# The causal mask moved from a matrix product to the row minimum, and q/k splits done for two heads at once, in a two-layer decoder trunk

## The chip, the cores and the metric

The kernel runs on one core of a Trainium2 chip. The metric is device microseconds of one execution of the whole program, the median of several. TensorE does the matrix products, VectorE, ScalarE and GpSimd the elementwise work, and SyncE issues the DMAs.

## The reference, cut to what matters

Two post-norm layers over 1024 tokens of width 1024. Layer 0 mixes tokens with differential attention, layer 1 with forgetting attention; each is followed by a gated MLP (2816 wide) with a causal convolution of width 3 on the gate branch. All is float32.

```python
def masked_softmax(scores, mask):
    s = jnp.where(mask, scores.astype(jnp.float32), -jnp.inf)
    return jax.nn.softmax(s, axis=-1)

# layer 0: 8 heads, each with 2 components of 64 dimensions
q = apply_rotary(...); k = apply_rotary(...)      # the first 16 dimensions of 64
s = jnp.einsum('bhcqd,bhckd->bhcqk', qb, k) * scale
p = masked_softmax(s, causal_mask(start, Q_BLOCK, S))
a = (p[:, :, 0] - lam * p[:, :, 1]).astype(v.dtype)
o = rms_norm(jnp.einsum('bhqk,bhkd->bqhd', a, v), subln_g) * (1.0 - lambda_init)

# layer 1: 16 heads of 64 dimensions, a forget gate per head and token
c = jnp.cumsum(log_f, axis=1).transpose(0, 2, 1)
s = (jnp.einsum('bhqd,bhkd->bhqk', qb, k) * scale + cb[..., :, None] - c[..., None, :])
p = masked_softmax(s, causal_mask(start, Q_BLOCK, S))

h = layer_norm(DEEPNORM_ALPHA * h + y, ...)       # y: attention output, then again the MLP's
```

## The kernel before, in words

**Float32 by halves.** A float32 factor is split into a high part, which TensorE's reduced float32 type holds exactly, and a low part, the rest. `split` (lines 83 to 91) does it: ScalarE copies the source into the high part (line 86), and VectorE subtracts that from the source (line 88, or line 90 where a scale is applied first). A float32 product is then three products, high x high, low x high and high x low (`mm3`, lines 97 to 99).

**Pairs.** The attention of a layer goes in 8 rounds (`attention`). A round works on two heads, in layer 0 on the two components of one head, and each of the two fills 64 of the 128 partitions. Round p does the scores, softmax and value products of pair p. Between them, in 48 steps of three products, it projects q, k and v of pair p + 1 (`project`, line 374), in halves of 512 tokens; in the last round the steps are products of the output projection. `tick`, `tock` and `steps` set how many steps stand between two score jobs. Work that must follow a projection is queued with a delay in steps (`after`, run by `pulse`): evacuation from PSUM one step later (`result`), and in layer 0 the DMAs that collect the rotary dimensions (`gather`), nine steps later the rotation (`turn`), fourteen later the split of q and k (`halves`). Weights come by DMA (`ahead`) and are split later (`ready`).

**Order.** Every engine takes its instructions in a fixed order, which a scheduler derives from the order in which the code is written. All DMAs of this part are issued by SyncE, on one queue, in order: a DMA that has to wait for an engine holds back those behind it.

**Scores.** For a pair there are five tiles of 128 x 1024: q of each head, with its high part on that head's 64 rows and its low part on the other 64 (`split_q`, two splits of 64 x 512 per half); k of each head, with the same high part on both halves of the rows, and one tile with the low parts of both (`split_k`, two splits and two ScalarE copies). Then `scores` (line 467) needs two products per 512 keys: the first (line 481) contracts high and low q together against the doubled high k, the second (line 482) high q, which GpSimd copies into a tile whose other rows are zero (`qz`, line 474), against low k. A third product (line 483) adds the mask, which is an identity times a 128 x 128 triangle, both bf16, to the diagonal block, the last 128 columns. Per layer that is 8 pairs x 2 heads x 8 query blocks = 128 score rows of 128 to 1024 keys.

**Softmax.** In layer 0 VectorE takes the negated row maximum (line 502), ScalarE the exponential. In layer 1 scores and mask have the opposite sign; VectorE adds the key's gate sum c, broadcast over 128 partitions by a DMA of 512 KB per head (`load_ck`), and takes the row minimum in one instruction (line 627), followed by a read of its accumulator into `nm`; two small subtractions (lines 629 and 630) take the query's gate sum in and out again. The gate sums themselves (`forget_sums`) are made early in layer 1 and go through DRAM (`cd`, line 598).

Of the kernel before, what the change touches and what calls it, by code (L numbers as in the profile page):

```python
# [19 lines left out]
P = 128  # L20
# [3 lines left out]
NP = 8  # L24
# [17 lines left out]
PIN = 1  # L42
PSF, PSN, PN17 = (0,), 3, 0
# [10 lines left out]
class Trunk:  # L54
# [64 lines left out]
    def consts(self):  # L119
# [5 lines left out]
        self.idb = cp.tile([P, P], BF16, name="idb")  # L125
        nc.vector.tensor_copy(self.idb, self.ident)
        self.mneg = cp.tile([P, P], BF16, name="mneg")
        nc.vector.tensor_copy(self.mneg, mask)
        self.mpos = cp.tile([P, P], BF16, name="mpos")
        nc.vector.tensor_scalar(self.mpos, mask, -1.0, None, op0=ALU.mult)  # L130
# [132 lines left out]
    def split_q(self, par, src, scale, sl):  # L263

        for st, r in zip(par, (0, 64)):
            self.split(st[r:r + 64, sl], st[64 - r:128 - r, sl], src[r:r + 64, :], scale)

    def split_k(self, par, src, sl):

        a, b, lo = par  # L270
        for st, r in ((a, 0), (b, 64)):
            s = src[r:r + 64, :]
            self.split(st[r:r + 64, sl], lo[r:r + 64, sl], s)
            self.nc.scalar.activation(st[64 - r:128 - r, sl], s, AF.Copy)


    def after(self, n, fn, *args):
        self.queue.append([n, partial(fn, *args)])

# [38 lines left out]
    def first_pair_rotary(self, t):  # L318
# [23 lines left out]
        for c in range(2):  # L342
# [7 lines left out]
            self.after(2 + 2 * c, self.turn_v, 0, c, dst[2], *t[5:], True)  # L350
        self.ahead(4)

    def first_pair(self, l, t):
# [4 lines left out]
        for c in range(2):  # L358
# [10 lines left out]
            if c:  # L369
                self.after(3, self.turn_v, l, c, dst, *t[5:], True)  # L370
            else:
                self.turn_v(l, c, dst, *t[5:])

    def project(self, l, p, t):
# [6 lines left out]
        for n, (s, c) in enumerate(order):  # L381
# [18 lines left out]
            if s == 2:  # L400
                self.after(D_EV + 2, self.turn_v, l, c, dst[2], *t[5:], True)
            if c:
                del self.w[i + s]

    def result(self, l, s, c, ps, dst, t):

        sl = slice(c * 512, c * 512 + 512)
        if dst is not None:
            self.nc.scalar.activation(dst[:, sl], ps, AF.Copy, scale=DH ** -0.5 if s == 0 else 1.0)
        elif s == 0:  # L410
            self.split_q(t[:2], ps, -DH ** -0.5, sl)
        else:
            self.split_k(t[2:5], ps, sl)

    def halves(self, dst, t, c):
        sl = slice(c * 512, c * 512 + 512)
        self.split_q(t[:2], dst[0][:, sl], None, sl)
        self.split_k(t[2:5], dst[1][:, sl], sl)
# [48 lines left out]
    def scores(self, q, kd, kl, r, qt, mask):  # L467
# [3 lines left out]
        h = r // 64  # L471
        qz = self.qz[h][self.nz[h] % 2]
        self.nz[h] += 1
        nc.gpsimd.tensor_copy(qz[r:r + 64, :], q[r:r + 64, qt * P:qt * P + P])  # L474
# [1044 lines left out]
```

## Time and profile before

| what | value |
| --- | --- |
| runs | 2517.57, 2517.7, 2519.43 us; median 2517.7 us |
| span of the profiled execution | 2518.0 us |
| TensorE busy over the span | 97% |
| layer 0's attention | about 45 to 535 us |
| layer 1's attention | about 1260 to 1805 us |
| SyncE issues | 244 MB on its queue |

The span is from the first to the last instruction of one execution. A row of the groups by line reads: line, engine, operation, output<-input by the program's names, partitions x elements and type, count; then busy time, mean ns of one; then the engine's idle time just before these instructions and what ended it. A row of the timeline reads: start, duration, engine, line, operation, and in brackets a wait that it ended. A row of the windows reads: the window, its length, then busy time and count for each engine.

### The profile page before, as it was taken

Reading aid. Unit: us, or ns where it says so; the run is one execution under the profiler, and the core shown is the slowest. Engines: PE = TensorE matmul, PEld = TensorE weight load, DVE = VectorE, ACT = ScalarE, POOL = GpSimd, SP = SyncE. Lnnn points to the kernel's source line nnn. Section 1 sums busy time; section 2 is a strip of 40 time slices with the busy share of each in tenths; the row PEclk is TensorE's granted clock in tenths of the full one; section 3 lists DMA queues with packets and bytes.
Section 4 is the critical chain, followed back from the end, with each engine's and each line's share of the span. In section 5 each row is a group of like instructions: output and inputs, shape, how many; then the busy total and the mean of one; then the engine's idle time right before and its main releaser. Section 6 shows DMA issues by size and latency. Waiting matters only on the chain. (4 is left out here: it accounts for less than half of the span.)

```text
span 2518.0 us, 33818 instructions
## 1 busy us (share of the span) xinstructions
PE 2450.5 (97%) x12059; PEld 2015.0 (80%) x12059; DVE 1966.9 (78%) x3794; ACT 1335.3 (53%) x2515; POOL 136.1 (5%) x314
## 2 busy tenths in 40 slices
PE   8999999999999999999999999999999999999998
PEld 6887777787888888878778888888877888888876
DVE  5787877989876676696868878888888667666978
ACT  5666666656544445434546656656465444445344
POOL 2001101101000000000100000000010000000000
PEclk9999999999999999999999999999999999999999
DMA  4111111422222223842311111114222222228622
GB/s 152 39 57 55 47 47 49 179 93 98 81 92 84 76 83 124 304 161 80 127 54 51 51 51 51 51 59 154 89 84 86 98 75 76 100 85 271 221 89 96
DMA packets 97402, 247.02 MB, mean 98 GB/s; under 512 B 14513, under 2 KB 21553, under 8 KB 97233
## 3 DMA queue, kind: packets, MB, share of 16 engines
q1 hardware_dynamic: 96720, 244.00, 28.3%
q8 instruction: 95, 1.56, 0.3%
q0 software_dynamic: 512, 0.85, 0.1%
q14 instruction: 75, 0.61, 0.1%
HBM read 190.93 MB, written 47.58 MB: 95 GB/s over the span
## 5 line engine op out<-in xcount | busy, mean ns | idle before, releaser
L97 PE MATMUL m<-xh,wh 128*128 128x512 f32 x768 | 321.5, 419 | 11.7 <-ACT xh L86 8.8
L98 PE MATMUL m<-xl,wh 128*128 128x512 f32 x768 | 303.4, 395 | 1.2 <-DVE xl L88 1.2
L99 PE MATMUL m<-xh,wl 128*128 128x512 f32 x768 | 304.0, 396 | 0.0
L97 PE MATMUL m<-xh,wo 128*128 128x512 f32 x656 | 255.6, 390 | 1.1 <-ACT pt L1029 0.7
L99 PE MATMUL m<-xh,wo 128*128 128x512 f32 x656 | 255.4, 389 | 0.3 <-DVE wo L88 0.3
L98 PE MATMUL m<-xl,wo 128*128 128x512 f32 x656 | 255.2, 389 | 0.0
L86 ACT ACTIVATE wo<-wg 128x512 fp32r<-128x512 f32 x168 | 106.4, 633 | 224.5 <-PE m L99 218.3
L97 PE MATMUL m<-q,wo 128*128 128x512 f32 x472 | 184.1, 390 | 0.0
L98 PE MATMUL m<-q,wo 128*128 128x512 f32 x472 | 183.8, 389 | 0.0
L99 PE MATMUL m<-q,wo 128*128 128x512 f32 x472 | 183.7, 389 | 0.0
L86 ACT ACTIVATE pt<-m 128x512 fp32r<-128x512 f32 (+1 forms) x240 | 129.5, 551 | 91.3 <-PE m L1303 71.2
L97 PEld LDWEIGHTS m<-xh,wh 128*128 128x128 f32 x768 | 145.7, 190 | 36.7 <-ACT xh L86 8.8
L99 PEld LDWEIGHTS m<-xh,wl 128*128 128x128 f32 x768 | 144.7, 188 | 31.2 <-DVE wl L88 0.6
L98 PEld LDWEIGHTS m<-xl,wh 128*128 128x128 f32 x768 | 145.6, 190 | 24.7 <-DVE xl L88 1.8
L86 ACT ACTIVATE wo<-t 128x512 fp32r<-128x512 f32 x132 | 82.7, 627 | 147.5 <-PE m L99 133.3
L88 DVE TENSOR_TENSOR pt<-m,pt 128x512 fp32r<-128x512 f32 (+1 forms) x240 | 149.6, 632 | 11.0 <-ACT pt L86 9.4
L88 DVE TENSOR_TENSOR wo<-wg,wo 128x512 fp32r<-128x512 f32 x168 | 115.4, 688 | 40.3 <-ACT wo L86 39.4
L97 PEld LDWEIGHTS m<-xh,wo 128*128 128x128 f32 x656 | 123.1, 188 | 27.7 <-ACT pt L1029 1.6
L99 PEld LDWEIGHTS m<-xh,wo 128*128 128x128 f32 x656 | 123.1, 188 | 26.7 <-DVE wo L88 1.2
L474 POOL CAST qz<-q 64x128 fp32r<-64x128 f32 x256 | 94.9, 372 | 910.1 <-PE s L483 832.8
L98 PEld LDWEIGHTS m<-xl,wo 128*128 128x128 f32 x656 | 123.1, 188 | 25.6
L86 ACT ACTIVATE oa<-ha 128x512 fp32r<-128x512 f32 x128 | 79.4, 624 | 112.6 <-PE s L99 57.7
(324 smaller groups left out, 6356.9 us busy)
## 6 DMA issues: line engine op xcount, KB each, us to landing
wst<-in_w SPq DMA_DIRECT2D x46, 512.0 KB, 3.3
t<-in_wi SPq DMA_DIRECT2D x44, 512.0 KB, 4.3
ad<-t SPq DMA_DIRECT2D x44, 512.0 KB, 3.5
ha<-ad SPq DMA_DIRECT2D x88, 256.0 KB, 5.5
wg<-in_wi SPq DMA_DIRECT2D x42, 512.0 KB, 3.3
wb<-in_wd SPq DMA_DIRECT2D x84, 256.0 KB, 3.3
pt<-in_wd SPq DMA_DIRECT2D x48, 256.0 KB, 3.8
wst<-in_wo SPq DMA_DIRECT2D x16, 512.0 KB, 3.3
```

Of the source, the lines that this page charges most:

```text
L86: nc.scalar.activation(hi, src, AF.Copy, scale=1.0 if scale is None else scale)
L88: nc.vector.tensor_tensor(lo, src, hi.bitcast(F32), op=ALU.subtract)
L97: mm(out, wh, xh, start=start, stop=False)
L98: mm(out, wh, xl, start=False, stop=False)
L99: mm(out, wl, xh, start=False, stop=stop)
L474: nc.gpsimd.tensor_copy(qz[r:r + 64, :], q[r:r + 64, qt * P:qt * P + P])
```

## The change

**Mask.** The third product goes in both layers. A constant tile `mask` of 128 x 1024 in bf16 holds zeros and, in its last 128 columns, the triangle. VectorE adds it to the scores and takes the row minimum in one instruction (`top`), the form that layer 1 had for its gate sums. Layer 0 now also has scores of the opposite sign, and its row maximum goes.

**Gate sums.** c is split into high and low part, and both go to DRAM. `load_c` brings the two rows of a head into rows 64 and 65 of the tile that holds this head's low k; the matching two rows of `qz` are ones, so the second score product contracts 66 rows and adds c. Each head of layer 1 thus has its own low tile with k on rows 0 to 63, the second being new (`kl`). The two small subtractions, the query's gate sum and the 16 broadcasts go.

**Splits.** `split_q` and `split_k` split both heads at once over 128 rows. `move_q` and `move_k` then bring the halves to where they belong, by DMAs of 64 x 512 from SBUF to SBUF: three for q and three for k per half of 512 tokens, in layer 1 four for k. They are queued two steps behind the split (`later`), and those of the first pairs are issued at once.

```diff
--- before
+++ after
@@ -40,6 +40,7 @@
 PIN = 1
+D_MV = 2
 PSF, PSN, PN17 = (0,), 3, 0
@@ -122,12 +123,9 @@
         nc.sync.dma_start(mask, i["mask"])
-        self.idb = cp.tile([P, P], BF16, name="idb")
-        nc.vector.tensor_copy(self.idb, self.ident)
-        self.mneg = cp.tile([P, P], BF16, name="mneg")
-        nc.vector.tensor_copy(self.mneg, mask)
-        self.mpos = cp.tile([P, P], BF16, name="mpos")
-        nc.vector.tensor_scalar(self.mpos, mask, -1.0, None, op0=ALU.mult)
+        self.mask = cp.tile([P, 1024], BF16, name="mask")
+        nc.gpsimd.memset(self.mask[:, :1024 - P], 0.0)
+        nc.vector.tensor_scalar(self.mask[:, 1024 - P:], mask, -1.0, None, op0=ALU.mult)
         self.qz = [[cp.tile([P, P], F32R, name=f"qz{h}{b}") for b in range(2)] for h in range(2)]
@@ -260,22 +258,48 @@
     def qtile(self, par):
         return self.qp.tile([P, 1024], F32R, tag=f"q{par}", name=self.nm("q"))
-    def split_q(self, par, src, scale, sl):
-        for st, r in zip(par, (0, 64)):
-            self.split(st[r:r + 64, sl], st[64 - r:128 - r, sl], src[r:r + 64, :], scale)
+    def split_q(self, par, src, lo, scale, sl):
+        x, y = par
+        self.split(x[:, sl], lo, src, scale)
+        return x[:, sl], y[:, sl], lo
+    def move_q(self, x, y, lo, l):
+        dma = lambda d, s: self.nc.sync.dma_start(d.bitcast(F32), s.bitcast(F32))
+        if l == 0:
+            dma(y[64:128], x[64:128])
+            dma(x[64:128], lo[0:64])
+            dma(y[0:64], lo[64:128])
+        else:
+            dma(y[0:64], x[64:128])
+            dma(x[64:128], lo[0:64])
+            dma(y[64:128], lo[64:128])
     def split_k(self, par, src, sl):
-        a, b, lo = par
-        for st, r in ((a, 0), (b, 64)):
-            s = src[r:r + 64, :]
-            self.split(st[r:r + 64, sl], lo[r:r + 64, sl], s)
-            self.nc.scalar.activation(st[64 - r:128 - r, sl], s, AF.Copy)
+        a, b, lo = [t[:, sl] for t in par[:3]]
+        self.split(a, lo, src)
+        return (a, b, lo, par[3][:, sl] if len(par) > 3 else None)
+    def move_k(self, a, b, lo, lo1):
+        dma = lambda d, s: self.nc.sync.dma_start(d.bitcast(F32), s.bitcast(F32))
+        dma(b[0:64], a[64:128])
+        dma(b[64:128], a[64:128])
+        dma(a[64:128], a[0:64])
+        if lo1 is not None:
+            dma(lo1[0:64], lo[64:128])
     def after(self, n, fn, *args):
         self.queue.append([n, partial(fn, *args)])
+    def later(self, fn, *args):
+        if self.fill is None:
+            fn(*args)
+        else:
+            self.after(D_MV, fn, *args)
     def step(self):
@@ -398,24 +422,28 @@
             if s == 2:
-                self.after(D_EV + 2, self.turn_v, l, c, dst[2], *t[5:], True)
+                self.after(D_EV + 2, self.turn_v, l, c, dst[2], *t[5:7], True)
             if c:
                 del self.w[i + s]
+            if l and c and s == 1:
+                self.after(D_EV + D_MV + 1, self.load_c, p, t)
     def result(self, l, s, c, ps, dst, t):
         if dst is not None:
-            self.nc.scalar.activation(dst[:, sl], ps, AF.Copy, scale=DH ** -0.5 if s == 0 else 1.0)
+            self.nc.scalar.activation(dst[:, sl], ps, AF.Copy, scale=-DH ** -0.5 if s == 0 else 1.0)
         elif s == 0:
-            self.split_q(t[:2], ps, -DH ** -0.5, sl)
+            lo = self.tp.tile([P, 512], F32R, tag="sq", name=self.nm("ql"), bufs=1)
+            self.later(self.move_q, *self.split_q(t[:2], ps, lo, -DH ** -0.5, sl), l)
         else:
-            self.split_k(t[2:5], ps, sl)
+            self.later(self.move_k, *self.split_k((*t[2:5], t[7]), ps, sl))
     def halves(self, dst, t, c):
         sl = slice(c * 512, c * 512 + 512)
-        self.split_q(t[:2], dst[0][:, sl], None, sl)
-        self.split_k(t[2:5], dst[1][:, sl], sl)
+        q, k = dst[0][:, sl], dst[1][:, sl]
+        self.later(self.move_q, *self.split_q(t[:2], q, q.bitcast(F32R), None, sl), 0)
+        self.later(self.move_k, *self.split_k(t[2:5], k, sl))
     def gather(self, dst, r, c):
@@ -464,24 +492,29 @@
                            v3[h][:, :, 64 - 64 * h:128 - 64 * h], t3[:, :, 64 * h:64 * h + 64])
-    def scores(self, q, kd, kl, r, qt, mask):
+    def scores(self, q, kd, kl, h, qt, l):
         nc = self.nc
-        h = r // 64
         qz = self.qz[h][self.nz[h] % 2]
         self.nz[h] += 1
+        r = 0 if l else 64 * h
         nc.gpsimd.tensor_copy(qz[r:r + 64, :], q[r:r + 64, qt * P:qt * P + P])
+        m = 66 if l else P
         ln = (qt + 1) * P
         for c in range((ln + 511) // 512):
-            n = min(512, ln - c * 512)
-            ks = slice(c * 512, c * 512 + n)
-            last = (c + 1) * 512 >= ln
+            ks = slice(c * 512, min(ln, c * 512 + 512))
             nc.tensor.matmul(sb[:, ks], q[:, qt * P:qt * P + P], kd[:, ks], start=True, stop=False)
-            nc.tensor.matmul(sb[:, ks], qz, kl[:, ks], start=False, stop=not last)
-        nc.tensor.matmul(sb[:, ln - P:ln], self.idb, mask, start=False, stop=True)
+            nc.tensor.matmul(sb[:, ks], qz[:m], kl[:m, ks], start=False, stop=True)
         return sb, ln
+    def top(self, sb, ln):
+        mn = self.small(tag="nm")
+        self.nc.vector.tensor_tensor_reduce(sb[:, :ln], sb[:, :ln], self.mask[:, 1024 - ln:], 1.0, BIG,
+                                            ALU.add, ALU.min, mn)
+        return mn
     def diff_jobs(self, p, t):
@@ -497,12 +530,11 @@
     def diff_scores(self, t, qt, j, pr, pts):
         nc = self.nc
-        sb, ln = self.scores(t[j], t[2 + j], t[4], 64 * j, qt, self.mneg)
-        nmx, lsum = self.small(tag="nm"), self.small(tag="ls")
-        nc.vector.tensor_reduce(nmx, sb[:, :ln], axis=AX.X, op=ALU.max, negate=True)
+        sb, ln = self.scores(t[j], t[2 + j], t[4], j, qt, 0)
+        mn, lsum = self.top(sb, ln), self.small(tag="ls")
         yield
         pt = self.tmp(pool=self.wp, tag="wst", bufs=2) if j else self.tmp(pool=self.pp, tag="p")
-        nc.scalar.activation(pt[:, :ln], sb[:, :ln], AF.Exp, bias=nmx, accum_out=lsum)
+        nc.scalar.activation(pt[:, :ln], sb[:, :ln], AF.Exp, bias=mn, scale=-1.0, accum_out=lsum)
         yield
@@ -586,7 +618,7 @@
         nc.vector.tensor_tensor_scan(c, self.ones, l, 0.0, op0=ALU.mult, op1=ALU.add)
-        self.c = c
+        self.c, self.cw8 = c, w
     def forget_sums(self):
@@ -594,17 +626,17 @@
         nc.vector.tensor_scalar(c, c, tb[:, 0:1], None, op0=ALU.add)
-        self.cd = self.dr.tile([16, 1024], F32, name="cd")
-        nc.sync.dma_start(self.cd.rearrange("h (b t) -> (h b) t", t=P), c)
-        tc = self.mbank()
-        nc.tensor.transpose(tc[:, :P], c, self.ident)
-        self.cq = self.cp.tile([P, 16, 8], F32, name="cq")
-        nc.vector.tensor_copy(self.cq.rearrange("p a b -> p (a b)"), tc[:, :P])
-    def load_ck(self, p, h):
-        ct = self.lp.tile([P, 1024], F32, tag="lg", name=self.nm("ck"))
-        self.nc.sync.dma_start(ct, self.cd[2 * p + h:2 * p + h + 1, :].broadcast_to([P, 1024]))
-        self.ck[p, h] = ct
+        self.cd = self.dr.tile([2, 16, 1024], F32, name="cd")
+        w = self.cw8
+        hl = [w[:, j * P:j * P + P].bitcast(F32R) for j in (5, 6)]
+        self.split(*hl, c)
+        for j in range(2):
+            nc.sync.dma_start(self.cd[j].rearrange("h (b t) -> (h b) t", t=P), hl[j].bitcast(F32))
+    def load_c(self, p, t):
+        for h in range(2):
+            self.nc.sync.dma_start(t[(4, 7)[h]][64:66, :].bitcast(F32), self.cd[:, 2 * p + h, :])
     def fox_jobs(self, p, t):
@@ -617,19 +649,8 @@
     def fox_scores(self, p, h, t, qt, pts):
         nc = self.nc
-        cq = self.cq[:, 2 * p + h, qt:qt + 1]
-        if qt == 0 and (p, h) not in self.ck:
-            self.load_ck(p, h)
-        ck = self.ck[p, h]
-        sb, ln = self.scores(t[h], t[2 + h], t[4], 64 * h, qt, self.mpos)
-        mn, lsum = self.small(tag="nm"), self.small(tag="ls")
-        nc.vector.tensor_tensor_reduce(sb[:, :ln], sb[:, :ln], ck[:, :ln], 1.0, BIG,
-                                       ALU.add, ALU.min, mn)
-        nc.vector.tensor_tensor(mn, cq, mn, op=ALU.subtract)
-        nc.vector.tensor_tensor(mn, cq, mn, op=ALU.subtract)
-        if qt == 7 and p < NP - 1:
-            self.load_ck(p + 1, h)
+        sb, ln = self.scores(t[h], t[2 + h], t[(4, 7)[h]], h, qt, 1)
+        mn, lsum = self.top(sb, ln), self.small(tag="ls")
         yield
@@ -653,12 +674,16 @@
         self.od = self.dr.tile([NP, P, 1024], F32, name=f"od{l}")
-        tiles = lambda p: [self.qtile((p + l) % 2) for _ in range(7)]
+        tiles = lambda p: [self.qtile((p + l) % 2) for _ in range(7)] + (
+            [self.lp.tile([P, 1024], F32R, tag="lg", name=self.nm("kl"))] if l else [])
         self.slabs = [self.i[f"w{l}"][s * NP + p] for p in range(NP) for s in range(3)]
         self.w, self.stage, self.queue = {}, {}, []
-        self.ofs, self.ck = {}, {}
+        self.ofs, self.fill = {}, None
         if l == 1:
+            for h in range(2):
+                for t in self.qz[h]:
+                    nc.gpsimd.memset(t[64:66, :].bitcast(F32), 1.0)
             self.gate_logits(0)
@@ -676,6 +701,7 @@
                         self.forget_sums()
+                        self.load_c(0, cur)
             total, acc, base = sum(j[0] + 1 + W_C for j in jobs) - (W_V * 10 if l == 0 else 0), 0, done
             def steps(goal):
```

In the tables of instructions below a name is a tile with its number; `L` is the line, which lies some 1 to 28 lines later after the change.

TensorE at the first score of layer 0 (`s` scores, `m` projection, `q` tiles of the pair, `ident,t` transposes of v). Before:

```order
L99 MATMUL m_514<-xh_258,wl_265 128x512
L481 MATMUL s_550<-q_117,q_115 128x128
L482 MATMUL s_550<-q_119,qz_278 128x128
L483 LDWEIGHTS idb
L483 MATMUL s_550<-mneg,idb 128x128
L97 MATMUL m_564<-xh_157,wh_510 128x512
```

After:

```order
L100 MATMUL m_511<-xh_258,wl_265 128x512
L98 MATMUL m_560<-xh_157,wh_507 128x512
L99 MATMUL m_560<-xl_158,wh_507 128x512
L100 MATMUL m_560<-xh_157,wl_508 128x512
L98 MATMUL m_560<-xh_161,wh_507 128x512
L99 MATMUL m_560<-xl_162,wh_507 128x512
L100 MATMUL m_560<-xh_161,wl_508 128x512
L478 MATMUL m_567<-ident,t_124 128x128 x3
L508 MATMUL s_547<-q_117,q_115 128x128
L509 MATMUL s_547<-q_119,qz_275 128x128
```

The mask product with its weight load is gone, and six products of the next projection and three transposes now stand ahead of the first score.

SyncE in round 3 of layer 0, from the rotation's return of the first half to the next weights (`t<-t` collects and returns rotary rows, `wst` weights). Before:

```order
L444 DMA t_2489<-t_2773 32x256 x2
L444 DMA t_2490<-t_2773 32x256 x2
L429 DMA t_2773<-t_2489 32x256
L431 DMA t_2773<-t_2489 16x256 x2
...
L106 DMA wst_2954<-in_w 128x1024
L429 DMA t_2773<-t_2490 32x256
L431 DMA t_2773<-t_2490 16x256 x2
```

After, with the moves of q (line 269) and k (line 287):

```order
L107 DMA wst_2890<-in_w 128x1024
L457 DMA t_2713<-t_2437 32x256
L459 DMA t_2713<-t_2437 16x256
L269 DMA q_2407<-q_2406 64x512
L269 DMA q_2407<-t_2437 64x512
L287 DMA q_2409<-q_2408 64x512 x2
L269 DMA q_2406<-t_2437 64x512
L459 DMA t_2713<-t_2437 16x256
L457 DMA t_2713<-t_2438 32x256
L287 DMA q_2408<-q_2408 64x512
L459 DMA t_2713<-t_2438 16x256 x2
L457 DMA t_2713<-t_2438 32x256
L459 DMA t_2713<-t_2438 16x256 x2
L107 DMA wst_2977<-in_w 128x1024
```

Six moves stand between and among the gathers of the second half, ahead of the weights that follow.

VectorE at two neighbouring scores of layer 1 (`ISA` is the add with minimum and, with `nm` alone, the read of its accumulator). Before:

```order
L627 ISA s_11980,nm_11984<-s_11980,ck_11977 128x128
L627 ISA nm_11984 128x1
L627 ISA s_11998,nm_12002<-s_11998,ck_11977 128x256
L627 ISA nm_12002 128x1
L629 TENSOR_TENSOR nm_11984<-cq,nm_11984 128x1
L629 TENSOR_TENSOR nm_12002<-cq,nm_12002 128x1
L630 TENSOR_TENSOR nm_11984<-cq,nm_11984 128x1
L630 TENSOR_TENSOR nm_12002<-cq,nm_12002 128x1
```

After:

```order
L91 SCALAR_TENSOR_TENSOR ql_13258<-m_13085,q_13042 128x512
L515 ISA s_13262,nm_13265<-s_13262,mask 128x512
L515 ISA nm_13265 128x1
L659 RECIPROCAL rs_13332<-ls_13267 128x1
```

The minimum is followed directly by other work, and the split of q covers both heads.

More of the change, by code (lines that the diff above doesn't have):

```diff
@@ L349, in first_pair_rotary @@
                 self.halves(dst, t, 1)
-            self.after(2 + 2 * c, self.turn_v, 0, c, dst[2], *t[5:], True)
+            self.after(2 + 2 * c, self.turn_v, 0, c, dst[2], *t[5:7], True)
         self.ahead(4)
@@ L369, in first_pair @@
             if c:
-                self.after(3, self.turn_v, l, c, dst, *t[5:], True)
+                self.after(3, self.turn_v, l, c, dst, *t[5:7], True)
             else:
-                self.turn_v(l, c, dst, *t[5:])
+                self.turn_v(l, c, dst, *t[5:7])
     def project(self, l, p, t):
```

## The prediction

> **What bounds the kernel now.** I read the page's head first, then the windows of the two attention stretches, then TensorE's timeline inside one of them, and only then the waits.
>
> ```profile
> span 2518.0 us, 33818 instructions
> PE 2450.5 (97%) x12059; PEld 2015.0 (80%) x12059; DVE 1966.9 (78%) x3794; ACT 1335.3 (53%) x2515; POOL 136.1 (5%) x314
> ...
> 45.00:535.00 490.00, 471.44 (x2566) 386.51 (x2565) 403.05 (x809) 316.01 (x674) 48.11 (x124) 1.00 0.21 69
> 1260.00:1805.00 545.00, 533.60 (x3062) 441.47 (x3061) 442.69 (x1173) 315.71 (x661) 42.26 (x124) 1.00 0.19 65
> ```
>
> The last two rows are the windows in which the mask products and the q/k splits run: layer 0's attention (490 us) and layer 1's (545 us). Columns are TensorE, weight loads, VectorE, ScalarE and GpSimd busy time, the granted clock (1.00), the share of the DMA engines (about a fifth) and GB/s. TensorE is busy 96% and 98% there, VectorE 82% and 81%, ScalarE 64% and 58%. So TensorE bounds both stretches. Matmuls overlap, so busy time does not price one; I price by the distance from one start to the next, in the timeline.
>
> **What the mask product costs.** The change takes all of them away:
>
> ```profile
> L483 PEld LDWEIGHTS <-idb x256: 95/95/99, 46.1 to 1801.6; 128*128 128x128 bf16 x128
> ...
> 301.87 0.23 PE L483 MATMUL s<-mneg,idb 128*128 128x128 bf16 x1
> 301.91 0.36 PE L97 MATMUL m<-pt,q 128*128 128x256 f32 x1
> 302.11 0.28 PE L98 MATMUL m<-pt,q 128*128 128x256 f32 x1
> 302.23 0.28 PE L99 MATMUL m<-pt,q 128*128 128x256 f32 x1
> ...
> 1505.06 0.23 PE L483 MATMUL s<-mpos,idb 128*128 128x128 bf16 x1
> 1505.10 0.48 PE L97 MATMUL m<-xh,wh 128*128 128x512 f32 x1
> 1505.41 0.39 PE L98 MATMUL m<-xl,wh 128*128 128x512 f32 x1
> 1505.64 0.40 PE L99 MATMUL m<-xh,wl 128*128 128x512 f32 x1
> ```
>
> The mask product itself (line 483) occupies only 0.04 us before the next start (301.87 to 301.91). But that next product then takes 0.20 us to its successor (301.91 to 302.11), where an equal one takes 0.12 (302.11 to 302.23). Together 0.24 us stand where 0.12 would. With a product of 512 columns behind it: 0.35 us (1505.06 to 1505.41) where 0.23 would stand (1505.41 to 1505.64). Both give 0.12 us per mask product. Reason, as I read it: its short run leaves too little time to load the next weights behind it. 256 x 0.12 = **31 us** less on TensorE. The lower bound is its own slot alone, 256 x 0.04 = 10 us; the upper is its whole modelled duration, 256 x 0.23 = 59 us, which the overlap contradicts. I take 31, since two spacings agree. The second score product of layer 1 now contracts 66 rows instead of 128; columns and count stay, and I give it nothing.
>
> The Trainium skill, page "TensorE: Matmul & The Clock Gate", section "Back-to-back issue gap", gives an isolated product of 128 columns 128/2.4 + 2.5 = 56 ns. By that the 256 would cost 14 us. The rows here show 0.12 us, so I go by the rows; the rule is the reading of a rival below.
>
> **VectorE and ScalarE.** The groups by line (last numbers: busy us, mean ns, idle before):
>
> ```profile
> L502 DVE TENSOR_REDUCE nm<-s 128x1 f32<-128x256 f32 (+7 forms) x128 | 96.3, 753 | 26.3 <-PE s L483 25.6
> L627 DVE CUSTOM_DVE_ANT_0 s<-s,ck 128x128 f32<-128x128 f32 (+7 forms) x128 | 97.1, 760 | 15.1 <-PE s L483 13.1 <-DMA ck<-cd 1.6
> L627 DVE DVE_READ_ACCUMULATOR2_ANT nm<- 128x1 f32 x128 | 17.3, 135 | 0.3
> L629 DVE TENSOR_TENSOR nm<-cq,nm 128x1 f32<-128x1 f32 x128 | 19.9, 156 | 2.3
> L630 DVE TENSOR_TENSOR nm<-cq,nm 128x1 f32<-128x1 f32 x128 | 20.5, 160 | 2.2
> ...
> L88 DVE TENSOR_TENSOR q<-t,q 64x512 fp32r<-64x512 f32 x64 | 43.9, 687 | 2.4 <-ACT q L86 0.4
> L90 DVE SCALAR_TENSOR_TENSOR q<-m,q 64x512 fp32r<-64x512 f32 x32 | 22.0, 689 | 5.3 <-ACT q L86 3.7
> L88 DVE TENSOR_TENSOR q<-m,q 64x512 fp32r<-64x512 f32 x32 | 22.0, 687 | 4.5 <-ACT q L86 3.7
> L88 DVE TENSOR_TENSOR q<-m,q 128x512 fp32r<-128x512 f32 x24 | 16.4, 683 | 0.0
> ...
> L86 ACT ACTIVATE q<-t 64x512 fp32r<-64x512 f32 x64 | 40.2, 628 | 1.8 <-DMA t<-t 0.8
> L274 ACT ACTIVATE q<-t 64x512 fp32r<-64x512 f32 x32 | 20.2, 631 | 0.8
> L86 ACT ACTIVATE q<-m 64x512 fp32r<-64x512 f32 x64 | 37.7, 589 | 24.4 <-DVE q L90 16.5 <-PE m L99 7.3
> L274 ACT ACTIVATE q<-m 64x512 fp32r<-64x512 f32 x32 | 19.0, 593 | 14.3 <-DVE q L88 14.1
> ```
>
> Layer 0's 128 row maxima (line 502) become the add-and-minimum that layer 1 already uses (line 627): 0.8 us more in all, plus 128 accumulator reads, 17.3 us. The mask operand is bf16 where ck was f32; no row shows that form, and I take the same duration. A split over 128 rows costs what one over 64 does (683 against 687 ns), so halving the count halves the time: 43.9/2 = 22 us off VectorE in layer 0 and 44/2 = 22 in layer 1. Layer 1 also loses lines 629 and 630, 40.4 us. VectorE: about -4 us in layer 0, -62 in layer 1. ScalarE had six passes per half pair and keeps two: 60.4 x 2/3 = 40 us off in layer 0, 56.7 x 2/3 = 38 in layer 1. None of this is on the path of a TensorE that is always fed. What it can give is a part of TensorE's idle time:
>
> ```profile
> L481 PE MATMUL s<-q,q 128*128 128x512 f32 (+3 forms) x384 | 132.2, 344 | 5.2 <-ACT wst L505 2.1 <-ACT p L635 1.3 <-ACT p L505 0.9
> L1303 PE MATMUL m<-ident,p 128*128 128x128 f32 x672 | 121.3, 279 | 9.9 <-DVE pt L88 4.0 <-DVE nm L630 2.6 <-DVE p L639 1.2
> L450 PE MATMUL m<-ident,t 128*128 128x128 f32 x128 | 19.6, 276 | 7.2 <-ACT t L409 5.8 <-DVE rs L508 1.4
> ```
>
> These 22 us wait for the probability chain or for an evacuation. I take **4 us** of it back (line 630's 2.6 vanish with the instruction, little besides). Bounds: 0, and half of TensorE's 30 idle us in both windows (490 - 471 and 545 - 534), 15.
>
> **The moves.** 208 DMAs of 64 x 512 floats (128 KB) come in, and 16 broadcasts of 512 KB leave. SyncE issues them in order, and a second hop (x's lower half to be overwritten only after it was copied) holds everything behind it until the first has landed.
>
> ```profile
> t<-t SPq DMA_DIRECT2D x128, 32.0 KB, 1.8
> wst<-in_w SPq DMA_DIRECT2D x46, 512.0 KB, 3.3
> ...
> 259.65 1.22 SPq L431 DMA_DIRECT2D t<-t  x2
> 260.92 0.58 SPq L106 DMA_DIRECT2D wst<-in_w  x1
> 265.99 0.51 SPq L429 DMA_DIRECT2D t<-t  x1
> 269.77 0.51 SPq L106 DMA_DIRECT2D wst<-in_w  x1
> ```
>
> Not shown before is a 128 KB move inside SBUF: between 1.8 us (32 KB) and 3.3 us (512 KB), I take 2. In layer 0's later pairs the six moves of the first half stand between the two gathers, where SyncE now has nothing from 261.5 to 266.0. Six issues of 0.6 us are 3.6, plus one wait of about 1 us for a hop: they fit, but one move stands among the k gathers behind 265.99 and shifts them and the weight load of 269.77 by 0.6 us. Queued behind are only those gathers, and the weight load has to be cut several microseconds later. So 0 us, unless a hop takes over 4 us (a rival). Layer 1 has no gathers; there the moves are alone with three weight loads a pair. The second half's moves run beside the next pair's short scores, which read only the first half.
>
> The first pair has no such cover:
>
> ```profile
> 45.22 0.58 SPq L106 DMA_DIRECT2D wst<-in_w  x1
> 45.91 0.22 PE L481 MATMUL s<-q,q 128*128 128x128 f32 x1
> ...
> 1293.84 0.33 SPq L598 DMA_DIRECT2D cd<-p  x1
> 1300.73 0.30 DVE L627 CUSTOM_DVE_ANT_0 s<-s,ck 128x128 f32<-128x128 f32 x1 [1.57 <-DMA ck<-cd]
> ```
>
> In layer 0 SyncE is solid with gathers up to 45.22. Six moves add 3.7 us there; the last hop lands at about 47.7. The order puts six projection products and three transposes (1.7 us) ahead of the first score (45.91), so it waits about 0.1. The weight load behind comes some 4 us later, and with it ScalarE's cut and the exponentials behind that cut: about 2 us (0 to 5). In layer 1 the second score product, on TensorE, now waits for the gate sums, where VectorE's add waited for the broadcast until 1300.73. Split of c (0.6 us) and a 2 us load of two rows against the 3.8 us broadcast: the same moment, but TensorE itself stands there: 1 us (0 to 3). Together **3 us**.
>
> **Sum.** 2518 - 31 - 4 + 3 = **2486 us**. The span is that of the profiled execution and lies within the three runs shown (2517.6 to 2519.4, median 2517.7), so nothing has to be added around it.
>
> **The rivals.**
>
> - *Own slot only.* The longer spacing behind the mask product has a cause that stays, such as the weight load behind a short last score product; then 0.04 to 0.056 us go (10 to 14 us): 2518 - 12 - 4 + 3 = 2505. For it: many of the last score products are 128 columns wide too. Against it: at 301.87 the last one is 512 wide.
> - *More than its own time.* With ScalarE 40 us lighter in each layer and VectorE 62 in layer 1, half of the idle 30 us goes: 2518 - 31 - 15 + 3 = 2475. Against it: the idle is in many short waits.
> - *VectorE becomes the bound of layer 0.* It gains nothing there (82% of 490 us) while each score waits 0.14 us longer for its exponential; if half of the 256 savings, those of layer 0, go into that: 2518 - 15.5 - 4 + 3 = 2502.
> - *SyncE holds the weights back.* If a hop takes over 4 us, the weight load behind the moves lands after its cut is due, ScalarE stands in front of its exponentials and TensorE runs dry. The price is in the waits view:
>
> ```profile
> ACT wh L86 <- DMA wst<-in_w: 18.1, 11, 3.2
> ```
>
>   The longest such wait is 3.2 us; at each of the 14 later pairs it makes 45 us: 2518 - 31 + 3 + 45 = 2535, slower than now. For it: this wait exists 11 times already. Against it: the free stretch on SyncE, and DMA engines that are four fifths idle.
>
> **Chances.** Forecast 0.58 (its own range 2476 to 2497), more than its own time 0.14, own slot only 0.10, VectorE 0.08, SyncE 0.10. The range 2468 to 2508 leaves out the SyncE case and the outer half of the second. About 0.2%, 5 us, is what a measurement can tell from no change here. Faster 0.87 (four cases, less a tail in which start-up costs eat the small ones), same 0.05, slower 0.08.
>
> **What would show it.** Right: TensorE's timeline has 0.12 us less behind each last score product, and both windows are shorter by about 15 us at the same idle. The moves land in about 2 us, and ScalarE's wait for weights stays below 20 us in all. Wrong: a spacing of 0.2 us that remains behind the last score product; TensorE idle that grows at scores with a DMA named as releaser; the first 60 us or the 50 us behind 1255 longer by more than 5 us.

## The result, and the profile after

The changed kernel takes 2485.8 us (median of four runs, 2482.1 to 2489.9), the kernel before 2517.6. The ratio is 0.9873, with a 95% interval of 0.9858 to 0.9889: 32 us less, with an uncertainty of about 4. The forecast was 2486 us. Its sum was right; two of its terms were not, and that their errors cancelled is luck.

The head of the page of the changed kernel:

```profile
span 2488.1 us, 33409 instructions
PE 2427.7 (98%) x11802; PEld 2019.7 (81%) x11802; DVE 1890.9 (76%) x3600; ACT 1254.8 (50%) x2388; POOL 134.4 (5%) x319
```

TensorE is still the bound. To see where the 30 us between the two spans lie, both traces are cut at the same events: at the first second score product of layer 0's round 1 (rounds count from 0), at the last one of layer 0, at the first of layer 1's round 1 and at the last of layer 1. Columns are as in the prediction's windows. Before:

```profile
0.00:100.65 100.65, 87.26 (x415) 70.14 (x415) 67.83 (x145) 59.90 (x116) 16.52 (x42) 1.00 0.36 112
100.65:528.37 427.72, 412.28 (x2256) 338.31 (x2255) 351.99 (x710) 274.64 (x593) 42.97 (x108) 1.00 0.21 72
528.37:1349.86 821.49, 808.80 (x3688) 661.08 (x3686) 622.60 (x1064) 396.50 (x682) 28.71 (x42) 0.99 0.32 110
1349.86:1801.35 451.49, 444.33 (x2585) 371.05 (x2584) 377.25 (x1001) 268.08 (x565) 36.88 (x108) 1.00 0.19 67
1801.35:2518.00 716.65, 697.78 (x3123) 574.40 (x3121) 547.22 (x878) 336.16 (x561) 11.00 (x14) 0.99 0.34 117
```

After:

```profile
0.00:100.03 100.03, 87.99 (x398) 70.89 (x399) 63.43 (x154) 51.40 (x103) 16.45 (x43) 0.99 0.50 141
100.03:510.56 410.53, 400.43 (x2146) 338.29 (x2145) 334.32 (x792) 243.17 (x541) 39.43 (x111) 1.00 0.33 99
510.56:1329.76 819.20, 807.11 (x3670) 661.36 (x3668) 613.09 (x1026) 387.23 (x667) 29.86 (x43) 0.99 0.34 113
1329.76:1769.13 439.37, 433.32 (x2475) 373.44 (x2473) 333.43 (x755) 236.71 (x517) 37.54 (x108) 0.99 0.27 80
1769.13:2488.10 718.97, 698.81 (x3122) 575.77 (x3120) 546.66 (x876) 336.28 (x561) 11.09 (x14) 0.99 0.34 117
```

Seven rounds of layer 0 give 17.2 us (427.7 to 410.5) and seven of layer 1 give 12.1 (451.5 to 439.4); the rest adds up to nothing (-0.6, -2.3 and +2.3). Each of the two stretches has lost 112 mask products. At 0.12 us these are 13.4 us, so layer 0 gained more than that and layer 1, as the rows stand, less.

The rows differ in one more thing, the granted clock of TensorE (the column before the DMA share). In these traces it is 1.00 but for stretches of some 3.4 or 6.8 us at 0.50, nearly all of them behind an idle time of TensorE, though not every idle time brings one (half-clock stretches in what follows). One lies in layer 1's rounds after (first two rows of windows, then TensorE's timeline):

```profile
1700.00:1705.80 5.80, 3.86 (x26) 3.46 (x26) 3.87 (x9) 2.59 (x7) 0.58 (x2) 1.00 0.89 317
1705.80:1712.60 6.80, 5.96 (x23) 5.38 (x23) 4.78 (x13) 4.86 (x13) 0.00 (x0) 0.50 0.03 14
...
1706.64 0.80 PE L98 MATMUL m<-wh,xh 128*128 128x512 f32 x1 [2.78 <-DVE pt L89]
...
1708.51 0.63 PE L99 MATMUL m<-wl,xh 128*128 128x512 f32 x1
1708.94 0.63 PE L100 MATMUL m<-wh,xl 128*128 128x512 f32 x1
...
1714.04 0.40 PE L100 MATMUL m<-wh,xl 128*128 128x512 f32 x1
1714.27 0.40 PE L98 MATMUL m<-wh,xh 128*128 128x512 f32 x1
```

Products of 512 columns follow each other after 0.43 us there (1708.51 to 1708.94), after 0.23 behind it (1714.04 to 1714.27). So half of such a stretch is lost, an estimate: 3.4 of the 439.4 us of layer 1's rounds. The row before has none, and of the ten kernels below that have no mask product, all with a full clock there, eight take 435.4 to 436.3 us and two 438.3 and 438.9. At equal clock layer 1 thus gains about 15.5 us and layer 0 about 18, both more than 13.4.

Most of the moves took 2.2 or 2.3 us from issue to landing, where the prediction had 2; those of q's low part in layer 1 took 4.2 (issues of the page: KB each, median us):

```profile
q<-q SPq DMA_DIRECT2D x128, 128.0 KB, 2.3
q<-t SPq DMA_DIRECT2D x32, 128.0 KB, 2.2
q<-ql SPq DMA_DIRECT2D x32, 128.0 KB, 4.2
```

### The profile page after: what moved, and what is told of

Its sections match the earlier page's. It is cut to its first block, busy times and chain, and to the rows that moved or that the text cites. A ratio compares the mean times of both kernels' runs of the same rounds, so it can differ in the third digit from the quotient of the medians.

```text
span 2488.1 us, 33409 instructions
## 1 busy us (share of the span) xinstructions
PE 2427.7 (98%) x11802; PEld 2019.7 (81%) x11802; DVE 1890.9 (76%) x3600; ACT 1254.8 (50%) x2388; POOL 134.4 (5%) x319
## 5 line engine op out<-in xcount | busy, mean ns | idle before, releaser
L515 DVE CUSTOM_DVE_ANT_0 s<-s,mask 128x128 f32<-128x128 f32 (+7 forms) x256 | 194.5, 760 | 47.3 <-PE s L509 45.7
```

The source lines that it names most:

```text
L515: self.nc.vector.tensor_tensor_reduce(sb[:, :ln], sb[:, :ln], self.mask[:, 1024 - ln:], 1.0, BIG, ALU.add, ALU.min, mn)
```

## The experiments

In what follows a difference is that of the medians from the changed kernel's 2485.8 us. Each kernel's ratio to the kernel before has an interval of about plus or minus 4 us, so differences below some 5 us are not told apart. Lengths of stretches are of one profiled execution each. The mean granted clock matters too: in the ten executions of the first kernel below it is 0.991 to 0.997, and 0.001 of it is 2.5 us of the span (an estimate, for a span that TensorE fills). Where it moves a reading, the text says so; "at equal clock" then means a difference with this taken off. The scheduler orders some instructions anew in each of these kernels. The diffs are shortened, and some comments in them stand for what the kernel says in more lines.

**The mask product put back without its use.**

```diff
-            nc.tensor.matmul(sb[:, ks], qz[:m], kl[:m, ks], start=False, stop=True)
+            nc.tensor.matmul(sb[:, ks], qz[:m], kl[:m, ks], start=False, stop=not last)
+        nc.tensor.matmul(sb[:, ln - P:ln], self.mask[:, :P], self.mask[:, P:2 * P], start=False, stop=True)
```

> The changed kernel with one more TensorE product per score row: 128 x 128 zeros times 128 x 128 zeros (bf16), added to the last 128 columns where the mask product stood (256 in all). VectorE still adds the mask. Theory (0.12 us per mask product on TensorE, 31 us in all, or some 28 after what stays behind the last score product): 2486 + 28 = 2514 us. Rival 'own slot only' (0.04 us each): 2486 + 10 = 2496 us. If the gain came from the lighter ScalarE and VectorE instead: 2488 us.

2506.9 us (2499.8 to 2513.6), ratio 0.996 [0.9948, 0.9972]: 21 us more. That is nearer to 28 than to 10. The rows by stage, then one place of TensorE's timeline in layer 1, for a score row whose last product is 128 wide (line 510; line 511 is the product of zeros):

```profile
98.52:521.32 422.80, 411.71 (x2256) 338.90 (x2255) 336.81 (x796) 244.26 (x544) 38.94 (x111) 1.00 0.32 97
1342.88:1789.71 446.83, 441.44 (x2585) 372.29 (x2584) 334.52 (x755) 237.24 (x517) 35.27 (x108) 1.00 0.27 79
...
1431.83 0.27 PE L510 MATMUL s<-q,qz 66*128 66x128 f32 x1
1431.95 0.23 PE L511 MATMUL s<-mask 128*128 128x128 bf16 x1
1431.99 0.48 PE L98 MATMUL m<-xh,wh 128*128 128x512 f32 x1
1432.30 0.39 PE L99 MATMUL m<-xl,wh 128*128 128x512 f32 x1
```

The same kind of place in the changed kernel:

```profile
1416.63 0.23 PE L508 MATMUL s<-q,q 128*128 128x128 f32 x1
1416.69 0.27 PE L509 MATMUL s<-q,qz 66*128 66x128 f32 x1
1416.80 0.45 PE L98 MATMUL m<-xh,wh 128*128 128x512 f32 x1
1417.09 0.40 PE L99 MATMUL m<-xl,wh 128*128 128x512 f32 x1
```

From the last score product to the second product behind it there are 0.47 us with the product of zeros and 0.40 without. Here the mask costs 0.07 us, not 0.12: a 128-wide score product has the same trouble as the mask product. It lasts 0.11 us to the next start where the equal-width product ahead of it lasts 0.06, and the 512-wide one behind it 0.29 where 0.23 is the rule. Over both traces, before and after, the medians of this distance differ by 0.12 us behind a last score product of 256, 384 or 512 columns, by 0.07 where a transpose follows, and by 0.07 behind one of 128 columns (a quarter of all). Weighted, the 256 come to some 26 us. The seven rounds of layer 0 show 12.3 us (422.8 against 410.5) and those of layer 1 7.5 us, 0.09 us per product over the 224; with the half-clock stretches taken out (in layer 0 1.7 us with the product of zeros and 0.7 without, in layer 1 none and 3.4) it is 11.3 and 10.9 us, 0.10 per product, as the spacings have it.

**The old splits, no moves.**

```diff
-        self.later(self.move_q, *self.split_q(t[:2], q, q.bitcast(F32R), None, sl), 0)
-        self.later(self.move_k, *self.split_k(t[2:5], k, sl))
+        self.split_q(t[:2], q, None, sl, 0)      # two splits of 64 rows, as before
+        self.split_k(t[2:5], k, sl)              # the same, and two copies by ScalarE
```

> The changed kernel with the splits of q and k as before (two of 64 x 512 per half and the copies by ScalarE) and no moves; mask and gate sums stay as changed. Theory (the relief of ScalarE and VectorE gives 4 us, the moves cost 3 at the start-ups and nothing in the rounds): 2486 + 4 - 3 = 2487 us. Rival 'more than its own time' (the lighter engines give back half of TensorE's idle time, 15 us): 2486 + 12 = 2498 us. Rival 'SyncE holds the weights back' in a small form (moves cost some us in every round): 2475 us.

2495.6 us, ratio 0.9918 [0.9904, 0.9933]: 10 us more. The wider splits with their moves are worth about 10 us, against the 1 (4 less 3) of the forecast. The clock hides a part: it is 0.996 in the mean of these executions and 0.994 in those of the changed kernel, and at equal clock the difference is some 15 us, an estimate.

**The wider splits and moves alone, on the kernel before.**

```diff
         else:
-            self.split_k(t[2:5], ps, sl)
+            self.later(self.move_k, *self.split_k(t[2:5], ps, sl))   # q and layer 0 likewise
```

> The kernel before with only the splits over 128 rows and the moves in both layers; mask product, row maximum and broadcast gate sums stay. Theory: 2518 - 4 + 3 = 2517 us. Rival 'more than its own time': 2518 - 15 + 3 = 2506 us. Rival 'SyncE holds the weights back': above 2530 us.

2507.8 us, ratio 0.9963 [0.9949, 0.9976]: 10 us below the kernel before. So the parts add up from either side: 10 us for the splits, 22 for the mask and the gate sums together (2517.5, the kernel before as measured beside it, to 2495.6 in the run above). Its rows by stage:

```profile
100.32:521.22 420.90, 411.69 (x2256) 339.00 (x2255) 333.38 (x685) 243.85 (x544) 38.98 (x108) 1.00 0.32 97
1340.30:1789.39 449.09, 442.38 (x2585) 371.95 (x2584) 362.41 (x977) 239.16 (x517) 37.75 (x108) 1.00 0.29 89
```

Layer 0's seven rounds fall by 6.8 us, those of layer 1 by 2.4.

**Every move twice.**

```diff
-        dma = lambda d, s: self.nc.sync.dma_start(d.bitcast(F32), s.bitcast(F32))
+        dma = lambda d, s: [self.nc.sync.dma_start(d.bitcast(F32), s.bitcast(F32)) for _ in range(2)]
```

> The changed kernel with each of the 208 moves issued twice. Theory: nothing in the later rounds, where SyncE is free; at the start of layer 0 six more issues of 0.6 us, and about 2 us in layer 1: 2486 + 5 = 2491 us. Rival 'SyncE holds the weights back': the wait for weights shows at most of the 14 later pairs, above 2505 us.

2498.0 us, ratio 0.9926 [0.9912, 0.994]: 12 us more, between the two expectations. In the trace, layer 0's round 1 begins 2.5 us later and its seven rounds are 6.2 us longer:

```profile
0.00:102.55 102.55, 89.48 (x399) 72.35 (x399) 60.56 (x150) 48.70 (x99) 16.53 (x43) 0.97 0.57 156
102.55:519.28 416.73, 401.02 (x2145) 339.23 (x2144) 336.43 (x794) 247.26 (x546) 39.59 (x111) 0.99 0.44 122
```

A second set of moves is thus not free in layer 0. But more than half of the 12 us goes with the clock: 0.991 in these executions against 0.994, some 7 us by the estimate above, and of the 8.7 us in the trace 5.1 are half-clock stretches (a 6.8 us one in the first row, another in the second). At equal clock some 5 us are left, as the theory expected, though it gave layer 0's rounds none of them. This prices the second set, not the first. ScalarE's wait for weights is no longer here than with single moves (26.9 and 28.4 us in the waits of the two), so the mechanism of the rival on SyncE is not what costs.

**ScalarE's saved time given back.**

```diff
-        nc.scalar.activation(hi, src, AF.Copy, scale=1.0 if scale is None else scale)
+        for _ in range(3):       # in the q and k splits alone
+            nc.scalar.activation(hi, src, AF.Copy, scale=1.0 if scale is None else scale)
```

> The changed kernel, where ScalarE writes the high part of each q and k split three times instead of once: 128 passes of 128 x 512, 0.63 us each, 80 us in all, which is what the wider splits took off ScalarE. Theory S (the 10 us that the wider splits and moves gave came from the lighter ScalarE): 2486 + 9 = 2495 us. Theory V (they came from VectorE): 2487 us. The first theory (4 us of relief in all): 2490 us at most.

2483.9 us, ratio 0.9863 [0.985, 0.9877]: no cost that the medians show. At equal clock (0.996 here) it is some 2 to 4 us, below the 9 of theory S, so ScalarE's relief gives little. As both extra passes stand ahead of VectorE's subtraction, the way from the rotation to the moves is also 1.3 us longer in each split, and that is within the same few microseconds.

**VectorE's saved time given back.**

```diff
+        if aliased:              # q of layer 0: its low part replaces the source
+            nc.vector.tensor_tensor(lo.bitcast(F32), src, src, op=ALU.max)
         for _ in range(1 if aliased else 2):     # in the q and k splits alone
             nc.vector.tensor_tensor(lo, src, hi.bitcast(F32), op=ALU.subtract)
```

> The changed kernel, where VectorE does one more pass of 128 x 512 in each q and k split: 64 passes of 0.69 us, 44 us in all, which is what the wider splits took off VectorE. Theory S (ScalarE gave the 10 us): 2487 us. Theory V: 2486 + 9 = 2495 us. The two together should make up the 10 us by which the run with the old splits was slower, plus the start-up that it saved.

2495.4 us, ratio 0.9913 [0.99, 0.9927]: 10 us more, as much as the old splits cost by the medians. At equal clock it is 11 of their 15, and ScalarE's few come on top. So most of what the wider splits gave is VectorE's. By stage:

```profile
102.82:522.93 420.11, 404.06 (x2145) 338.64 (x2144) 347.58 (x819) 242.86 (x541) 39.86 (x111) 1.00 0.33 97
522.93:1342.16 819.23, 806.71 (x3669) 661.36 (x3668) 617.55 (x1033) 386.78 (x667) 29.48 (x43) 0.99 0.34 113
1342.16:1778.49 436.33, 431.39 (x2474) 370.97 (x2473) 345.98 (x779) 236.34 (x517) 36.73 (x108) 1.00 0.28 81
```

All of it lies in layer 0: its seven rounds take 420.1 us against 410.5, and round 1 begins 2.8 us later, while layer 1 is not longer with as much added (436.3 against 439.4, which is 436.0 without the half-clock stretch). One thing stays open: with the old splits the largest sum among TensorE's waits in layer 0 is for evacuations by ScalarE (6.7 us), here no wait for them is left, so the two cost alike without waiting alike.

**No moves for the first pairs.** The first pair of each layer is split as before; all others as changed.

```diff
+        if self.fill is None:
+            self.old_q(t[:2], q, None, sl, 0)
+            return self.old_k(t[2:5], k, sl)
```

> The changed kernel with the old splits, and so no moves, for the first pair of each layer alone; all later pairs as changed. Theory: the start of layer 0 is 2 us shorter (first score at 46.0 us, not 47.8) and that of layer 1 up to 1 us: 2486 - 3 = 2483 us. Rival (the start hides in other waits of the first pairs): 2486 us.

2488.9 us, ratio 0.9888 [0.9875, 0.9902]: no gain. Round 1 of layer 0 begins at 102.6 us, not at 100.0, although the second product of the first score is 2.3 us earlier (45.5 against 47.8): what the start gains is lost within the first round. Of its 2.6 us more, 1.9 are half-clock stretches (an estimate), one of them behind TensorE's idle 2.6 us at 51.8; in this round VectorE and ScalarE again have the more numerous passes.

```profile
0.00:102.59 102.59, 87.95 (x398) 71.77 (x399) 67.33 (x158) 56.80 (x111) 17.26 (x43) 0.97 0.42 123
```

**The moves issued by GpSimd.**

```diff
-        dma = lambda d, s: self.nc.sync.dma_start(d.bitcast(F32), s.bitcast(F32))
+        dma = lambda d, s: self.nc.gpsimd.dma_start(d.bitcast(F32), s.bitcast(F32))
```

> The changed kernel with the moves issued by GpSimd in place of SyncE. If the moves on SyncE's queue cost in the later rounds, as the run with moves twice suggests (12 us for 208 more): 2486 - 8 = 2478 us. If they are free there and only the start-up counts: 2484 us. Rival: GpSimd copies the q block that the second score product waits for, and an issue or a hop ahead of that copy holds TensorE: above 2490 us.

2507.9 us, ratio 0.9964 [0.995, 0.9977]: 22 us more, and all of it in layer 0, whose seven rounds take 433.1 us. The waits show a chain that the prediction had given to SyncE (the first two rows are of the whole trace, the last of layer 0 alone; columns: total us, times, longest):

```profile
ACT wh L87 <- DMA wst<-in_w: 51.2, 16, 5.8
POOL q L269 <- ACT q L87: 102.2, 28, 18.2
...
PE m L478 <- ACT t L435: 18.3, 6, 4.2
```

GpSimd stands in front of moves whose splits are not done; ScalarE waits 51 us for weights (28.4 in the changed kernel), and TensorE 18 us for evacuations by ScalarE, up to 4.2 us at a time. Behind five of these six waits the granted clock is 0.50 for 3.4 or 6.8 us, so that some 10 of the 433.1 us are lost to the clock, against 0.7 in the changed kernel: a long wait of TensorE is paid for twice. Why the weights come later here, though SyncE has fewer issues, was not tried.

**Two small VectorE operations behind each row minimum.**

```diff
+        for _ in range(2):
+            self.nc.vector.tensor_scalar(mn, mn, 0.0, None, op0=ALU.add)
         return mn
```

> The changed kernel with two small VectorE operations (add of zero, 128 x 1, 0.16 us each) behind each row minimum in both layers: 512 of them, 41 us in each layer; in layer 1 they stand where the two subtractions of the gate sums were. Theory V2 (VectorE nearly bounds layer 0 and not layer 1: 22 us more on it cost 11.5 us in layer 0's rounds and none in layer 1's): layer 0 longer by some 20 us, layer 1 by under 5: 2486 + 22 = 2508 us. Rival (what counts is the length of VectorE's long passes, and small operations hide): below 2492 us. Rival (VectorE counts in both layers alike): 2486 + 40 = 2526 us.

2491.8 us, ratio 0.9898 [0.9883, 0.9913]: 6 us more, a quarter of what theory V2 expected, and nothing in layer 1 (436.3 us). By stage, then VectorE's timeline in layer 0 (line 518 is the small operation):

```profile
98.43:515.56 417.13, 402.28 (x2145) 337.22 (x2144) 351.32 (x1018) 245.36 (x543) 46.11 (x111) 1.00 0.32 97
1333.36:1769.63 436.27, 431.59 (x2475) 370.83 (x2473) 359.58 (x977) 239.39 (x517) 39.29 (x108) 1.00 0.27 81
...
302.61 0.15 DVE L518 TENSOR_SCALAR nm<-nm 128x1 f32<-128x1 f32 x1
302.68 0.68 DVE L89 TENSOR_TENSOR pt<-m,pt 128x512 fp32r<-128x512 f32 x1
303.28 0.14 DVE L518 TENSOR_SCALAR nm<-nm 128x1 f32<-128x1 f32 x1
303.34 0.41 DVE L467 TENSOR_TENSOR t<-t,rope 128x256 f32<-128x256 f32 x1
```

The theory had the load too large: an operation lasts 0.15 us, but the next one starts 0.07 us behind its start in the median. VectorE's busy time in the seven rounds of layer 0 grows by 17 us, not by the 36 that its expectation gives for them, and 6.6 of these 17 show in the length. That small operations hide better than long ones is not shown.

**A pass of layer 0 moved from VectorE to ScalarE.**

```diff
-            nc.vector.tensor_scalar(pt[:, :ln], pt[:, :ln], rs, None, op0=ALU.mult)
+            nc.scalar.activation(pt[:, :ln], pt[:, :ln], AF.Copy, scale=rs)
```

> The changed kernel, in layer 0 with the scaling of the first component's probabilities by its row sum (64 passes, 34 us on VectorE) done by ScalarE. Theory V2: VectorE is relieved where it counts, and 80 us more on ScalarE cost nothing: of the 34 us a third to a half come back, as far as TensorE's 19 us of longer waits in layer 0 allow: 2486 - 10 = 2476 us. Rival (the relief is used up with the change; what TensorE waits for now is latency): 2486 us. Rival (ScalarE's exponentials come later): above 2490 us.

2488.0 us, ratio 0.9885 [0.9869, 0.9902]: no gain, at equal clock either. In the seven rounds VectorE is busy 22 us less than in the changed kernel, and the rounds are as long:

```profile
97.64:508.94 411.30, 399.52 (x2146) 337.59 (x2144) 312.20 (x741) 278.26 (x600) 38.78 (x111) 1.00 0.34 100
```

**The extra VectorE pass in one half of layer 0's splits.** As above, in the second half of the tokens alone, whose splits stand at the border of two rounds, and in the first half alone.

```diff
-        self.split(a, lo, src)
+        self.split(a, lo, src, None, 1, 2 if len(par) == 3 and sl.start == 512 else 1)   # layer 0; or 0; q likewise
```

> The changed kernel with VectorE's extra pass of 128 x 512 in the q and k splits of layer 0's second half alone (16 passes, 11 us on VectorE); these splits stand at the border between two rounds, where TensorE waits for the transposes' probabilities. Theory B (VectorE decides at the border of the rounds only): most of the 10 us that the extra passes in all splits cost: 2486 + 8 = 2494 us. Rival (any VectorE work in layer 0 counts alike): 2486 + 5 = 2491 us. Rival (none of it counts alone): 2487 us.

> The same with the extra pass in the splits of layer 0's first half alone (16 passes, 11 us), which stand in the middle of a round. Theory B: 2487 us. Rival (any VectorE work in layer 0 counts alike): 2491 us.

2490.4 us, 0.9903 [0.9889, 0.9916], and 2491.8 us, 0.9911 [0.9894, 0.9927]: 5 and 6 us more, at the edge of what the runs tell from nothing. The border of the rounds is nothing special; each half costs about half of the 10 us. Theory B falls.

Put together, the seven rounds of layer 0 in the kernels without a mask product (the two with other moves left out):

| VectorE busy, us | length, us | kernel |
| --- | --- | --- |
| 312 | 411.3 | a pass moved to ScalarE |
| 334 | 410.5 | as changed |
| 335 | 410.2 | no moves for the first pairs |
| 336 | 412.3 | ScalarE's time given back |
| 341 | 419.4 | extra pass, first half |
| 343 | 416.2 | extra pass, second half |
| 348 | 420.1 | extra pass, both halves |
| 351 | 417.1 | small operations |
| 355 | 422.4 | old splits |

With the half-clock stretches taken out (an estimate) the lengths are, from the top, 411.3, 409.8, 409.7, 412.3, 418.5, 416.2, 418.4, 417.1 and 422.4 us. Up to some 336 us, 82% of the stretch, VectorE's load changes little; above, the rounds are 6 to 12 us longer. Nine single executions don't tell whether that is a slope of about a half or a step between 336 and 341 us, and the last row has a heavier ScalarE too. In layer 1 the length of its seven stays between 435 and 440 us from 333 to 360 us of VectorE, which is 82% too. Whether a like point lies farther up there is open: with the mask product the stretch takes 446.8 us at 335 us of VectorE, 449.1 at 362, and 451.5 at the 377 of the kernel before.

## Why the prediction was right, point by point

**What bounds.** TensorE does, but not alone. Averages of 82% and 81% made VectorE look alike in both layers; in layer 0 its load was past the point from which it counts, in layer 1 hardly.

**The mask product** (31 us, 0.12 us each) was the right mechanism and the wrong size: putting it back cost 21 us, the spacings give 26. The failing step is "I take 31, since two spacings agree". At the first place, 301.87, the last score product is 512 columns wide; at the second, 1505.06, it is 128 wide, as this row of the trace before shows:

```profile
1504.94 0.28 PE L482 MATMUL s<-q,qz 128*128 128x128 f32 x1
```

There the 0.23 us that the prediction took as the rest is not what is left without the mask. Behind a 128-wide last score product, and ahead of a transpose, 0.05 of the 0.12 us stay, since, as I read it, that product leaves as little time for the next weights. The rival "own slot only" (10 to 14 us) named just these products but took its price for all. What separates 21 from 26 lies within the uncertainty of the runs; at equal clock the two stretches show 0.10 us per product, which is 26 for the 256.

**VectorE and ScalarE** (4 us) gave about 10, more at equal clock. The step that failed is "None of this is on the path of a TensorE that is always fed", for layer 0; TensorE's idle time in its rounds fell from 15.4 to 10.1 us, where the prediction looked for the same idle. The waits of TensorE that were to show this name the instruction that released it, mostly evacuations by ScalarE, but ScalarE's load was little of the cause: with its 80 us back the median did not rise, with VectorE's 44 back it rose by 10 us. The two subtractions of layer 1, from which most of the 4 us were taken, cost nothing that can be measured when like operations are put in their place. The rival "more than its own time" had this effect at 15 us, with half of the idle time taken back. The rival "VectorE becomes the bound of layer 0" had the place but started from the wrong side, as did "about -4 us in layer 0": VectorE is busy 352 us before and 334 after in the seven rounds. The wider splits take off 18.6 us (333.4 in the run with them alone), and minimum and accumulator reads, priced at 18 us for the eight rounds, add only 0.9 to that (to 334.3). The price came from the lengths of the records: from the start of the row maximum, or of the add with its read behind it, to the next instruction's start, where that does not wait, the medians differ by about 0.01 us at every width (0.734 and 0.743 at 640 columns).

**The moves** (0 in the later pairs) can't be priced apart from the splits that they make possible; together they gain 10 us. A second set costs 12 us, some 7 of them with the lower clock; which wait brings the rest was not found, and SyncE's room is not shown to be the reason. "ScalarE's wait for weights stays below 20 us in all" was wrong (28.4 us, 14 times, from 18.1), but hardly reached TensorE, whose own waits for these weights come to 0.2 us; in the run with GpSimd's queue, at 51 us, TensorE's waits for ScalarE grew with it.

**The start-up** (3 us) was seen where it was predicted: the second product of layer 0's first score starts at 47.8 us, 1.9 later. But round 1 starts 0.6 us earlier than before, and without the moves of the first pair 2.6 later than with them (0.6 at equal clock). The cost is paid back within the first round. In layer 1 TensorE's waits name no DMA, and the stretch that holds its start is 2.3 us shorter. So the term is 0.

In sum: -22 for the mask and the gate sums and -10 for the splits and moves make -32, where the prediction had -31, -4 and +3. The bound and the main mechanism were right; the exact sum was luck.

## What to carry to other kernels

Price a short product by what starts late behind it, and then look at what is left when it is gone: a short neighbour brings the same delay. Price small operations of VectorE by the next start too, not by the length of the record. Where two engines are above 80% in a stretch, put a known load on the other and see whether the time moves, in each stage by itself; before reading a few microseconds, compare the granted clock of the stretches; the engine named in the waits need not be the one whose load matters. And splitting work over all 128 partitions and moving halves by DMA paid here although the moves themselves were not free.

## What was not expected of the hardware

- Of two 128-wide float32 products in a row, the first lasts 0.06 us to the next start, the second 0.11, and a 512-wide one behind them 0.29 in place of 0.23: the delay comes one product late.
- An add with row minimum against a bf16 mask takes 760 ns in the mean of 256, the same as against float32 gate sums (760 ns of 128):

```profile
L515 DVE CUSTOM_DVE_ANT_0 s<-s,mask 128x128 f32<-128x128 f32 (+7 forms) x256 | 194.5, 760 | 47.3 <-PE s L509 45.7
```

- 80 us of extra ScalarE work cost at most some 4 us (it is then busy 66% of layer 0's rounds), 44 us of extra VectorE work cost 10 us (then 83%).
- A wait of TensorE can cost more than its length: behind waits of 2.8 to 4.2 us the granted clock was 0.50 for 3.4 or 6.8 us.
